# Moving six products in a feed-forward stage and reordering two accumulating transfers in a gate stage

## The chip, the cores and the metric

The kernel runs on one core of a Trainium2 chip. Such a core has a matrix engine (TensorE, PE in the profile, with its weight loads as PEld), three engines for element-wise work (VectorE or DVE, ScalarE or ACT, GpSimd or POOL), and a queue engine (SyncE or SP) that here only issues transfers. POOL also issues transfers. Every engine works through its own list of instructions in a fixed order and waits on semaphores for what others produce. The metric is the device time of one execution in microseconds (us). Three executions of the kernel before took 872.46, 872.75 and 873.51 us; the median, 872.75, is the time to compare with.

## The reference

One transformer-like layer on a sequence of 512 tokens with 1024 channels, in float32. Cut to what matters here:

```python
h = rms_norm(x, norm_mix)
u_pool, u_lru, q, k, v, g_logits = jnp.split(h @ w_in, splits, axis=-1)
gates = jax.nn.sigmoid(g_logits + b_gate).reshape(B, S, 3, D_MODEL)
merged = (gates[:, :, 0] * (y_pool @ w_branch[0])      # causal pooling mixer
          + gates[:, :, 1] * (y_lru @ w_branch[1])     # gated linear recurrence
          + gates[:, :, 2] * (y_sb @ w_branch[2]))     # stick-breaking attention
x = x + merged @ w_out
h2 = rms_norm(x, norm_ffn)
x = x + (silu(h2 @ w_ffn_gate) * (h2 @ w_ffn_up)) @ w_ffn_down
```

The change touches two places: the product that makes the third branch's gate logits (`gates[:, :, 2]`), and the first part of `silu(h2 @ w_ffn_gate) * (h2 @ w_ffn_up)`, where the feed-forward width of 2816 is worked through in 11 chunks of 256.

## The kernel before

**Precision.** Each float32 operand is split into a rounded high part and a low remainder: ACT copies the operand to the rounded type, DVE subtracts (L141 and L142, or L1442 and L1443 in the feed-forward chunks). A product is then three matmuls: high by high, high by low, low by high. So each weight tile costs one ACT and one DVE instruction before PE can use it. The split weights live in rotating buffers, three for the high and three for the low parts (`whi`, `wlo`); a fourth split waits until PE has finished with the first.

**Seven products instead of eight.** Some matrix products are done by a Strassen-like scheme: a 2x2 block product with seven block products, named 11, 12, S2, S1, S3, S4 and 22 after the weight block or sum of blocks that they use, in this order. The weight sums are made on the way. For the third branch's gate weights (two blocks, units 3 and 4 of the loader, `add_seven`), the sums are made partly by transfers: a load brings block "21", and an accumulating transfer from POOL's queue adds block "22" into it (L200). Later, when block "11" has been split and DVE has read it for another sum (L217), an accumulating transfer from POOL's queue adds "21" into the tile of "11" (L218); the result is the operand of product S3. When unit 3's block "11" has been handled, the loader also calls for unit 4's "21" and "11" (L223): SP issues the loads (L198), and POOL the addition L200 for unit 4.

**The feed-forward chunks.** The first two of the eleven chunks (`NDIRECT = 2`) use plain products with an activation that is not yet divided by its root mean square. Their results in PSUM are `pg` (gate) and `pu` (up). For each half j of a chunk, DVE multiplies `pg[j]` by 1/rms (L1513), ACT takes Silu (L1514), DVE multiplies by `pu[j]` (L1515) and by 1/rms again (L1516). The other nine chunks, `seven(c)`, use the seven-product scheme. There the weight sums S3, S2, S1 and S4 are made by DVE (L1424) from the loaded blocks, in buffers of which three rotate, and then split (L1442, L1443). `make_a(upto)` makes operands up to a count, three products ahead of the one that PE gets next: before chunk 2's first product, 11, 12 and S2 are made; S1 is made at the second product, S3 at the third, and so on. PSUM is used in four buffers of two banks each (`fp`); in chunk 2 the buffers of `pg` and `pu` of chunk 1 are the other two, and chunk 3's products take them.

**What sets the order.** The kernel is written as a program in Python, and a planner turns it into one fixed list for each engine. It simulates the engines with a cost for every instruction. Earlier instructions in the program have precedence, blocks under `tc.high_priority` more; but when an engine is free, the planner gives it what is ready by its simulation, so a later instruction that is ready can come ahead of an earlier one that is not. On the chip the list is then kept whatever the real times are. `tc.issue_after(ins)` makes the instructions of a block that go to the queue of `ins` stand behind `ins` in that list; it waits for nothing else.

Of the kernel before, what the change touches and what calls it, by code (L numbers as in the profile page):

```python
# [12 lines left out]
ALU = mybir.AluOpType  # L13
# [16 lines left out]
NDIRECT = 2  # L30
# [37 lines left out]
def layer_kernel(ctx: ExitStack, tc: tile.TileContext, x, xt, vecs, w_in, w_qkv7, w_gate7, w_pool, w_rg, w_ig,  # L68
                 w_branch, w_br7, w_out, w_fg, w_fu, w_fd, w_fd7, out):
    nc = tc.nc  # L70
# [14 lines left out]
    def b4(shape, name, tag="b", dt=F32):  # L85
        bufs = {"w": NAW, "t": NAT, "b": NAB}[tag]
        return pools["ap0"].tile([P] + shape, dt, tag=tag, name=name, bufs=bufs)
# [28 lines left out]
    def in_order2(ap):  # L116
        if ap.shape[-1] == H:
            return ap.rearrange("p w (b a) -> p w a b", a=2)
        return ap.rearrange("p w (c b a) -> p (w c) a b", c=2, a=2)

    def two2(ap):
        if ap.shape[-1] == H:
            return ap.rearrange("p w (a b) -> p w a b", a=2)
        return ap.rearrange("p w (c a b) -> p (w c) a b", c=2, a=2)
# [9 lines left out]
    def split_w(raw, shape, n, o=0):  # L134
        hi, lo = weight_tiles("whi" + n, "wlo" + n, o)
        if len(shape) == 3:
            hi, lo = (t.rearrange("p (a b) -> p a b", a=shape[1]) for t in (hi, lo))
        else:
            hi, lo = (t.rearrange("p (a b c) -> p a b c", a=shape[1], b=shape[2]) for t in (hi, lo))
        with tc.high_priority(60):  # L140
            act(hi, raw, AF.Copy)  # L141
            dve.tensor_tensor(lo, raw, hi.bitcast(F32), ALU.subtract)  # L142
        return hi, lo
# [42 lines left out]
    def seven_src(u, nm, i):  # L186
        if u < 3:
            return w_qkv7[u, CH[nm], KH[nm], i]
        return w_gate7[u - 3, CH[nm], KH[nm]]

    def seven_load(n, nms):
        if n >= len(UNITS):
            return
        u, pieces, shape = UNITS[n]
        for nm in nms:
            for i in range(pieces):
                qraw[u, nm, i] = r = b4(list(shape), f"qw{u}{nm}{i}", "w")
                nc.sync.dma_start(r, seven_src(u, nm, i))  # L198
                if nm == "21":
                    nc.gpsimd.dma_start(r, seven_src(u, "22", i), accum_op=ALU.add)  # L200

    def add_seven(un, nm, i):
        u, pieces, shape = UNITS[un]
        last = i == pieces - 1

        def make(n):
            if nm == "S4":
                r = qraw[u, "12", i]
                dve.tensor_tensor(r, r, qraw[u, "S2", i], ALU.add)
            src = qraw[u, {"S1": "21", "S3": "11", "S4": "12"}.get(nm, nm), i]  # L210
            o = 0
            if u >= 3:
                o = goffs.pop(0) if goffs else OFF
            parts = split_w(src, [P] + list(shape), n, o)
            if nm == "11":
                qraw[u, "S2", i] = r = b4(list(shape), f"qs{u}{i}")
                dve.tensor_tensor(r, qraw[u, "21", i], src, ALU.add)  # L217
                nc.gpsimd.dma_start(src, seven_src(u, "21", i), accum_op=ALU.add)  # L218
            if last:
                if un < 3:  # L220
                    seven_load(un + 1, {"S1": ("21",), "S3": ("11",), "S4": ("12",), "22": ("22",)}.get(nm, ()))
                elif un == 3:
                    seven_load(un + 1, {"11": ("21", "11"), "12": ("12",), "S2": ("22",)}.get(nm, ()))  # L223
            return parts
        specs.append((("seven", u, nm, i), make))

# [86 lines left out]
    def product(a_, b_, ps, half, first, last, ws=(0, 1)):  # L313
        for w in ws:
            o = ps[:, w, half * H:(half + 1) * H]
            for k in range(4):
                for n, (a, b) in enumerate(((0, 0), (0, 1), (1, 0))):
                    nc.tensor.matmul(o, a_[a][:, w, k, :], il2(b_[b][:, k, :]),  # L318
                                     start=first and n == k == 0,
                                     stop=last and n == 2 and k == 3, skip_group_check=True)  # L320
# [39 lines left out]
    def tick(n=1):  # L360
        for _ in range(n):
            if abg:
                abg.pop(0)()
            for _ in range(1 + (len(bg) > 8 and "many" in state)):
                if bg:
                    bg.pop(0)()
# [29 lines left out]
    def chan_chunk(key, rhs, nticks=0, pool=None, pair=False):  # L396
        pss = chunk_psum(key, pool, pair)
        for half in range(2):
            half_chunk(pss if type(pss) is list else [pss[:, j, :] for j in range(2)], key, half, rhs,
                       nticks)  # L400
        return pss
# [39 lines left out]
    with ExitStack() as first:  # L441
# [449 lines left out]
        for cc in range(2):  # L891
# [14 lines left out]
            for nm in ORDER:  # L906
                ps, half, first_, t, ts_, src, ss = plan[nm]
# [387 lines left out]
    with ExitStack() as ffn:  # L1295
        gp = ffn.enter_context(tc.tile_pool(name="gp", bufs=GBUFS))

        def g4(shape, name, dt=F32):

            return gp.tile([P] + shape, dt, tag="g", name=name)  # L1300

        def small(name, bufs=1, tag=None, dt=F32):
            return gp.tile([P, S], dt, tag=tag or name, name=name, bufs=bufs)
# [122 lines left out]
        def make_a(upto):  # L1426
            while made[0] < min(upto, len(steps)):
                c, nm = steps[made[0]]
                made[0] += 1
                if (c, nm) == (NDIRECT, "11"):  # L1430
                    offs.extend(STEPS)
                while made[1] < min(c + 2, DOWN):
                    load_a(made[1])
                    made[1] += 1
                sums_a(c, nm)
                A[c, nm] = split_a(raw[c, nm], f"{c}_{nm}")
# [30 lines left out]
        def finish_act(t, ps, a):  # L1467

            v = two2(t)
            dve.tensor_tensor(v, v, in_order2(ps), ALU.add)  # L1470
            act(t[:, 0, :], t[:, 0, :], AF.Silu)
            dve.tensor_tensor(a, t[:, 0, :], t[:, 1, :], ALU.mult)
# [4 lines left out]
        def seven(c):  # L1477
            a = g4([2, S], f"act{c}")
            tx, ty = g4([2, S], f"tx{c}"), g4([2, S], f"ty{c}")
            Y = fp.tile([P, 2, S], F32, tag="mm", name=f"ps_y{c}")  # L1480
            X = fp.tile([P, 2, S], F32, tag="mm", name=f"ps_x{c}")
            lo, hi = slice(0, H), slice(H, S)
            plan = (("11", Y, 1, True, tx, lo, Y, hi),
                    ("12", X, 0, True, None, None, None, None),
                    ("S2", Y, 1, False, tx, hi, Y, hi),
                    ("S1", X, 1, False, ty, hi, X, hi),
                    ("S3", Y, 1, False, ty, lo, Y, hi),
                    ("S4", X, 1, False, None, None, None, None),
                    ("22", Y, 0, False, None, None, None, None))
            n0 = steps.index((c, "11"))  # L1490
            for n, (nm, ps, half, first, t, ts_, src, ss) in enumerate(plan):
                make_a(n0 + n + 3)
                product(A.pop((c, nm)), B[0, WITH[nm]], ps, half, first, True)
                if t is not None:
                    act(two2(t[:, :, ts_]), in_order2(src[:, :, ss]), AF.Copy)
                if c == DOWN - 1 and nm in PRE:
                    split_d2("11", PRE.index(nm), 0, 0)
                if nm == "S4":
                    finish_act(tx, X, a[:, 0, :])
                if nm == "22":  # L1500
                    finish_act(ty, Y, a[:, 1, :])
            acts.append(a)

        bg.extend([lambda: None, rms2] + prepare_b())
        for c in range(NDIRECT):
            pg = chan_chunk(("fg", c), h2, 3, fp)
            pu = chan_chunk(("fu", c), h2, 3, fp)
            if c == NDIRECT - 1:
                make_a(3)
            a = g4([2, S], f"act{c}")  # L1510
            for j in range(2):
                sg = small(f"sg{c}{j}", 2, "sq2")
                dve.tensor_tensor(two(sg), in_order(pg[j]), two(rb2), ALU.mult)  # L1513
                act(sg, sg, AF.Silu)  # L1514
                dve.tensor_tensor(two(sg), two(sg), in_order(pu[j]), ALU.mult)  # L1515
                dve.tensor_tensor(a[:, j, :], sg, rb2, ALU.mult)  # L1516
            acts.append(a)
        tick(len(bg))
        for c in range(NDIRECT, NF // 2):
            if c == NF // 2 - 1:  # L1520
                ah, al = g4([2, S], "ah", F32R), g4([2, S], "al", F32R)
                act(ah, acts[0], AF.Copy)
                dve.tensor_tensor(al, acts[0], ah.bitcast(F32), ALU.subtract)
            seven(c)
# [207 lines left out]
```

## Time and profile before

| | us |
|---|---|
| median of 3 executions | 872.75 |
| the profiled execution | 872.6 |
| its span (first to last instruction) | 870.8 |
| PE busy in the span | 859.7 (99%) |
| DVE busy | 741.2 (85%) |
| ACT busy | 522.1 (60%) |
| POOL busy | 91.8 (11%) |

The span is divided, in order of time, into the first gates and the recurrence (to about 143 us), the attention inputs and the third branch's gates (to about 283), pooling, attention and the branch projections (to about 506), the output projection (to about 550), the feed-forward chunks (about 550 to 762) and the down projection. The gate stage of the first edit lies at 250 to 283 us, the feed-forward place of the second at 582 to 613 us.

Three things help in reading the rows. A row of a timeline gives the start, the duration, engine, line, operation and tiles, and in brackets how long the engine was idle before it and who ended that. Matmuls overlap: a matmul of 256 columns is shown with 0.28 us, but the next one starts 0.11 us later, so a loss on PE is read from the distance of starts, not from the busy time. A transfer's row on POOL or SP is only its issue; the time to landing is shown in the chain of waits or in the views of transfers.

### The profile page before, as it was taken

What the parts mean: (1) busy time and instruction counts of PE and PEld (TensorE: products, weight loads), DVE (VectorE), ACT (ScalarE), POOL (GpSimd) and SP (SyncE); (2) the same over time, 40 slices, a digit from 0 to 9 for tenths busy, and PEclk for the clock granted to TensorE, in tenths of its full rate; (3) what the DMA queues carried; (4) which work ended last, traced back from release to release, by engine and by line L of the source; (5) the groups of instructions that cost most, each with busy time, mean ns of one, the idle gap of its engine ahead of it and who ended that gap; (6) DMA issues with size and microseconds to landing.
All of it is one profiled execution on the core that took longest, in us unless ns stands there. A gap on an engine that the chain in (4) does not pass through costs nothing.

```text
span 870.8 us, 14268 instructions
## 1 busy us (share of the span) xinstructions
PE 859.7 (99%) x5563; PEld 789.7 (91%) x5563; DVE 741.2 (85%) x961; ACT 522.1 (60%) x727; POOL 91.8 (11%) x130
## 2 busy tenths in 40 slices
PE   9999999999999999999999999999999999999998
PEld 7888878888899888889889998889999999999998
DVE  7899897998787699977898786699988888899974
ACT  6554989556856565565665545464555555755642
POOL 1110002232433101000001100000000000121200
PEclk9999999999999999999999999999999999999999
DMA  9686356799582786635736955345543343798913
GB/s 340 167 291 195 97 169 194 215 318 253 176 271 73 238 246 205 218 122 155 217 98 152 212 171 170 98 138 151 150 117 97 106 114 109 233 243 204 192 39 121
DMA packets 116643, 154.08 MB, mean 177 GB/s; under 512 B 8160, under 2 KB 90080, under 8 KB 116576
## 3 DMA queue, kind: packets, MB, share of 16 engines
q1 hardware_dynamic: 103904, 107.30, 38.5%
q0 software_dynamic: 12528, 45.62, 22.1%
q8 instruction: 43, 0.70, 0.3%
q10 hardware_dynamic: 144, 0.26, 0.1%
q14 instruction: 24, 0.20, 0.1%
HBM read 132.71 MB, written 18.87 MB: 174 GB/s over the span
## 4 chain that ended last, share of the span: by engine, by line
PE 76%; DVE 10%; ACT 6%; DMA 4%; issue 2%; SPq 1%; POOL 0%; ACTq 0%; DVEq 0%; POOLq 0%
PE ps_y L318 10%; PE ps_x L318 8%; PE ps_q L834 6%; PE ps_dy L1651 6%; PE ps_dx L1651 5%; DVE wlo L142 3%; PE ps_br L309 3%; PE ps_br L310 3%; PE ps_br L311 3%; PE ps_bY L1277 2%; PE ps_gate L737 2%; DMA qw<-in_w_gate_dram 2%; PE ps_bX L1277 2%; ACT whi L141 2%; PE ps_gy L318 2%
## 5 line engine op out<-in xcount | busy, mean ns | idle before, releaser
L141 ACT ACTIVATE whi<-raw 128x1024 fp32r<-128x1024 f32 x69 | 72.8, 1055 | 76.8 <-PE ps_out L310 16.0
L142 DVE TENSOR_TENSOR wlo<-raw,whi 128x1024 fp32r<-128x1024 f32 x69 | 84.2, 1220 | 23.6 <-ACT whi L141 23.0
L142 DVE TENSOR_TENSOR wlo<-qw,whi 128x1024 fp32r<-128x1024 f32 x48 | 58.4, 1219 | 17.3 <-ACT whi L141 17.1
L141 ACT ACTIVATE whi<-qw 128x1024 fp32r<-128x1024 f32 x48 | 50.4, 1052 | 29.9 <-PE ps_q L834 14.9
L1442 ACT ACTIVATE wh_S<-w_S 128x1024 fp32r<-128x1024 f32 x36 | 38.0, 1059 | 33.0 <-PE ps_y L318 19.9
L1555 POOL DMA_DIRECT2D dw<-in_w_down_dram x20 | 16.9, 862 | 306.3 <-DMA dw<-in_w_down_dram 263.8
L1443 DVE TENSOR_TENSOR wl_S<-w_S,wh_S 128x1024 fp32r<-128x1024 f32 x36 | 43.7, 1220 | 3.8 <-ACT wh_S L1442 3.8
L1442 ACT ACTIVATE wh<-w 128x1024 fp32r<-128x1024 f32 x27 | 28.6, 1058 | 26.9 <-issue 9.1
L1443 DVE TENSOR_TENSOR wl<-w,wh 128x1024 fp32r<-128x1024 f32 x27 | 32.9, 1220 | 8.4 <-ACT wh L1442 8.4
L1442 ACT ACTIVATE whdS<-dw 128x1024 fp32r<-128x1024 f32 x20 | 21.2, 1058 | 21.3 <-PE ps_dy L1651 10.6
L1443 DVE TENSOR_TENSOR wldS<-dw,whdS 128x1024 fp32r<-128x1024 f32 x20 | 24.2, 1220 | 5.5 <-ACT whdS L1442 5.5
L1093 DVE TENSOR_TENSOR_SCAN E<-K,ahead 128x512 f32<-128x512 f32 (+3 forms) x32 | 25.3, 812 | 3.9 <-ACT K L1089 3.9
L309 PE MATMUL ps_br<-yHH,whi 128*128 128x512 f32 x64 | 24.6, 385 | 1.4 <-ACT up L980 1.4
L309 PE MATMUL ps_lru<-HH,whi 128*128 128x512 f32 x64 | 24.6, 384 | 0.0
L309 PE MATMUL ps_br<-yph,whi 128*128 128x512 f32 x64 | 24.5, 383 | 0.0
L309 PE MATMUL ps_pool<-HH,whi 128*128 128x512 f32 x64 | 24.5, 383 | 0.0
L309 PE MATMUL ps_gate<-HH,whi 128*128 128x512 f32 x64 | 24.4, 381 | 0.0
L310 PE MATMUL ps_br<-ypl,whi 128*128 128x512 f32 x64 | 24.3, 379 | 0.0
L311 PE MATMUL ps_gate<-HH,wlo 128*128 128x512 f32 x64 | 24.3, 379 | 0.0
L310 PE MATMUL ps_gate<-HL,whi 128*128 128x512 f32 x64 | 24.3, 379 | 0.0
L310 PE MATMUL ps_br<-yHL,whi 128*128 128x512 f32 x64 | 24.3, 379 | 0.0
L311 PE MATMUL ps_br<-yHH,wlo 128*128 128x512 f32 x64 | 24.3, 379 | 0.0
(740 smaller groups left out, 3444.1 us busy)
## 6 DMA issues: line engine op xcount, KB each, us to landing
raw<-in_w_in_dram SPq DMA_DIRECT2D x31, 512.0 KB, 5.1
qw<-in_w_qkv_dram SPq DMA_DIRECT2D x24, 512.0 KB, 7.0
dw<-in_w_down_dram POOLq DMA_DIRECT2D x20, 512.0 KB, 7.6
w<-in_w_ffn_gate_dram SPq DMA_DIRECT2D x36, 256.0 KB, 3.6
w<-in_w_ffn_up_dram SPq DMA_DIRECT2D x36, 256.0 KB, 4.5
raw<-in_w_branch_dram SPq DMA_DIRECT2D x16, 512.0 KB, 3.9
qw<-in_w_qkv_dram POOLq DMA_DIRECT2D x12, 512.0 KB, 8.0
qd<-r POOLq DMA_DIRECT2D x12, 512.0 KB, 7.4
```

The source lines that it names most:

```text
L141: act(hi, raw, AF.Copy)
L142: dve.tensor_tensor(lo, raw, hi.bitcast(F32), ALU.subtract)
L309: nc.tensor.matmul(ps, lh, rh, start=start, stop=False, skip_group_check=skip)
L310: nc.tensor.matmul(ps, lh, rl, start=False, stop=False, skip_group_check=skip)
L311: nc.tensor.matmul(ps, ll, rh, start=False, stop=stop, skip_group_check=skip)
L318: nc.tensor.matmul(o, a_[a][:, w, k, :], il2(b_[b][:, k, :]), start=first and n == k == 0, stop=last and n == 2 and k == 3, skip_group_che ...
L834: nc.tensor.matmul(ps[:, a, :], b_[:, k, ts_], il(a_[:, kk, :]), start=first and n == k == 0, stop=n == 2 and k == 3, skip_group_check=True)
L1093: dve.tensor_tensor_scan(E[:, c0:c0 + n][:, ::-1], K[:, c0 + 1:c0 + n + 1][:, ::-1], ahead[:, S - n:][:, ::-1], 0.0, ALU.mult, ALU.add)
L1277: nc.tensor.matmul(o, ah[x_][:, w, k, :], il2(b[k][y_]), start=first_ and n == k == 0, stop=n == 2 and k == 3, skip_group_check=True)
L1442: act(h, src, AF.Copy)
L1443: dve.tensor_tensor(l, src, h.bitcast(F32), ALU.subtract)
L1651: nc.tensor.matmul(o, a_[a][:, w, k0 + k, :], il2(b_[b][:, k, :]), start=first and i == k == 0, stop=last and i == 2 and k == nk - 1, skip ...
```

## The change

First, in the loader: where unit 3's "11" is handled, the transfers for unit 4's "21" and "11" are traced inside `tc.issue_after` of the accumulating transfer L218. So POOL's addition for the second gate block (L200) stands behind POOL's addition for the first (L218). SP's loads are not affected, being on another queue.

Second, in the feed-forward stage: the instructions that L1513 to L1516 stand for become a function of the half j, `direct_act(j)`. For chunk 0 it is called where the lines stood. For chunk 1 it is called inside `seven(2)`: for half 0 behind the second product ("12"), for half 1 behind the third ("S2"). No instruction is added or removed.

```diff
@@ in add_seven
-                nc.gpsimd.dma_start(src, seven_src(u, "21", i), accum_op=ALU.add)
+                add = nc.gpsimd.dma_start(src, seven_src(u, "21", i), accum_op=ALU.add)
             if last:
                 if un < 3:
                     seven_load(un + 1, {"S1": ("21",), "S3": ("11",), "S4": ("12",), "22": ("22",)}.get(nm, ()))
+                elif un == 3 and nm == "11":
+                    with tc.issue_after(add.ins):
+                        seven_load(un + 1, ("21", "11"))
                 elif un == 3:
-                    seven_load(un + 1, {"11": ("21", "11"), "12": ("12",), "S2": ("22",)}.get(nm, ()))
+                    seven_load(un + 1, {"12": ("12",), "S2": ("22",)}.get(nm, ()))
@@ in seven(c), end of the loop over the seven products
                     finish_act(ty, Y, a[:, 1, :])
+                if (c, n) in after:
+                    after[c, n]()
@@ the direct chunks
             a = g4([2, S], f"act{c}")
-            for j in range(2):
+
+            def direct_act(j, c=c, a=a, pg=pg, pu=pu):
                 sg = small(f"sg{c}{j}", 2, "sq2")
                 dve.tensor_tensor(two(sg), in_order(pg[j]), two(rb2), ALU.mult)
                 act(sg, sg, AF.Silu)
                 dve.tensor_tensor(two(sg), two(sg), in_order(pu[j]), ALU.mult)
                 dve.tensor_tensor(a[:, j, :], sg, rb2, ALU.mult)
+
+            if c < NDIRECT - 1:
+                direct_act(0), direct_act(1)
             acts.append(a)
         tick(len(bg))
+        after = {(NDIRECT, 1): lambda: direct_act(0), (NDIRECT, 2): lambda: direct_act(1)}
```

## The prediction

> **What bounds the kernel now.** I read the page first, for the busy engine and the clock; then the waits of TensorE (PE); then, at the two waits that the diff touches, PE's timeline, the chain of waits, and the timelines of the queues that come last there.
>
> ```profile
> span 870.8 us, 14268 instructions
> PE 859.7 (99%) x5563; PEld 789.7 (91%) x5563; DVE 741.2 (85%) x961; ACT 522.1 (60%) x727; POOL 91.8 (11%) x130
> PEclk9999999999999999999999999999999999999999
> ```
>
> The whole span is PE's at full clock. No matmul is added or removed, so the change can only remove or create moments in which PE stands still. The waits of PE, for the places that matter:
>
> ```profile
> PE ps_br L309 <- ACT up L980: 1.4, 1, 1.4
> PE ps_x L318 <- DVE wl_S L1443: 0.8, 1, 0.8
> PE ps_gy L318 <- ACT gx L910: 0.5, 1, 0.5
> ```
>
> The second row lies in the feed-forward chunk whose neighbour the diff edits, the third in the gate block whose additions it reorders. The view of waits counts idle time of a modelled span; PE's own rows give the loss in starts:
>
> ```profile
> 261.07 0.28 PE L318 MATMUL ps_gx<-hT1h,wlo 128*128 128x256 f32 x1
> 261.84 0.38 PE L318 MATMUL ps_gy<-hT3h,whi 128*128 128x256 f32 x1 [0.50 <-ACT gx L910]
> 262.06 0.28 PE L318 MATMUL ps_gy<-hT3l,whi 128*128 128x256 f32 x1
> ...
> 601.00 0.28 PE L318 MATMUL ps_y<-B0T2h,wl_S 128*128 128x256 f32 x1
> 601.40 0.38 PE L318 MATMUL ps_x<-B0T1h,wh_S 128*128 128x256 f32 x1
> 601.61 0.28 PE L318 MATMUL ps_x<-B0T1l,wh_S 128*128 128x256 f32 x1
> 602.66 0.38 PE L318 MATMUL ps_x<-B0T1h,wl_S 128*128 128x256 f32 x1 [0.77 <-DVE wl_S L1443]
> 602.87 0.28 PE L318 MATMUL ps_x<-B0T1h,wh_S 128*128 128x256 f32 x1
> ```
> ```profile
> 238.85 7.23 DMA qw<-in_w_gate_dram
> 248.72 10.48 DMA qw<-in_w_gate_dram
> 264.79 2.68 PE ps_gx L318 x24
> ```
>
> The last fence is the chain of waits from 225 to 300 us; its row of 24 matmuls gives the undisturbed step, 2.68 / 24 = 0.11 us. In the gate block two steps took 262.06 - 261.07 = 0.99 us instead of 0.22: 0.77 us lost. In the chunk four steps took 602.87 - 601.00 = 1.87 us instead of 0.44: 1.43 us lost. These two sums, 2.20 us, are all that the change can take away directly.
>
> **Edit 1, the order of two additions on POOL.** In the loader, the first gate block's "11" step adds "21" into its own tile (L218, needed for product S3). The loads for the second block follow, with an addition of their own (L200). The rows of DVE, POOL and ACT from the timeline (start, duration, line, tiles, idle time before and who ended it):
>
> ```profile
> 242.58 1.22 DVE L217 TENSOR_TENSOR qs<-qw,qw 128x1024 f32<-128x1024 f32 x1
> 246.68 0.88 POOL L200 DMA_DIRECT2D qw<-in_w_gate_dram  x1 [10.39 <-DMA qw<-in_w_gate_dram]
> 247.28 1.76 POOL L787 DMA_DIRECT2D qd<-r  x2
> 248.72 1.28 POOL L218 DMA_DIRECT2D qw<-in_w_gate_dram  x1
> 262.67 1.22 DVE L217 TENSOR_TENSOR qs<-qw,qw 128x1024 f32<-128x1024 f32 x1
> 259.30 2.00 ACT L141 ACTIVATE whi<-qw 128x1024 fp32r<-128x1024 f32 x2 [3.57 <-DMA qw<-in_w_gate_dram]
> 261.21 0.58 ACT L910 ACTIVATE gx<-ps_gy 128x512 f32<-128x512 f32 x1
> ```
>
> POOL was idle for 10.39 us ahead of L200, until the load of 238.85 had landed at 246.08; L218 had its inputs when DVE's L217 read the tile for the last time, at 242.58 + 1.22 = 243.80, and stood behind it. It went out at 248.72 and landed 10.48 later, at 259.20. ACT, in its order, waited 3.57 us for that landing, did two weight roundings, and only then the snapshot gx at 261.21, whose end releases PE's S3. From landing to PE: 261.84 - 259.20 = 2.64 us.
>
> With the edit L218 goes out at about 243.85, when POOL is idle. With the same 10.48 us it lands at 254.3. PE could go on at 261.07 + 0.11 = 261.18, which needs a landing by 261.18 - 2.64 = 258.54: 4.2 us to spare. What then ends ACT's wait is the buffer rotation, not the load. So the 0.77 us go. Behind L218 now stand L200 and the two stores L787. L200 has to wait until 246.08 for its load anyway; even if it lands 10.48 us after its old start, at 257.2, its reader, the second block's own L217 (the row at 262.67), came 5 us later. The stores are read after 290 us. SP issues the same loads in the same order and waits for nothing new. Cost nothing, gain 0.77; bounds 0 (it lands late all the same) and 0.77.
>
> ```profile
> 236.00:244.00 8.00, 8.00 (x39) 7.00 (x38) 7.09 (x7) 6.12 (x7) 0.29 (x1) 1.00 1.02 306
> 244.00:254.00 10.00, 10.00 (x63) 9.20 (x62) 9.97 (x9) 5.38 (x6) 3.96 (x5) 1.00 0.92 267
> DMA to landing us min/median/max: 5.2/7.5/11.2
> ```
>
> The first two rows are busy time by stretch (their last two numbers: share of the DMA engines, GB/s), the third belongs to the qw tile's POOL transfers. The 16 DMA engines were full when L218 would now start, so it joins a crowd; the longest landing of any such transfer was 11.2 us, and 243.85 + 11.2 = 255.1 is still before 258.54. The Trainium skill, page "DMA: Bandwidth & Descriptors", section "Issuing engines are not separate DMA queues", says that transfers issued from different engines run on the same 16 DMA engines and interleave. By that rule the earlier addition shares with SP's loads instead of going after them, which speaks against this edit; the trace agrees in so far as the share is at 1.02 with both in flight.
>
> **Edit 2, six products moved on DVE.** For chunk 1 (the second direct one) DVE did, for each half j, L1513, L1515 and L1516, with ACT's Silu between; now half 0 is queued after product "12" of chunk 2 and half 1 after "S2". None is removed. DVE before, from the timeline:
>
> ```profile
> 592.55 1.22 DVE L1424 TENSOR_TENSOR w_S<-w,w 128x1024 f32<-128x1024 f32 x1
> 593.69 0.68 DVE L1513 TENSOR_TENSOR sg<-ps_fg,rb 128x512 f32<-128x512 f32 x1
> 594.29 1.21 DVE L1424 TENSOR_TENSOR w_S<-w,w_S 128x1024 f32<-128x1024 f32 x1
> 595.42 0.68 DVE L1515 TENSOR_TENSOR sg<-sg,ps_fu 128x512 f32<-128x512 f32 x1
> 596.02 0.68 DVE L1513 TENSOR_TENSOR sg<-ps_fg,rb 128x512 f32<-128x512 f32 x1
> 596.70 1.22 DVE L1443 TENSOR_TENSOR wl_S<-w_S,wh_S 128x1024 fp32r<-128x1024 f32 x1
> 597.84 0.68 DVE L1516 TENSOR_TENSOR act<-sg,rb 128x512 f32<-128x512 f32 x1
> 598.44 0.68 DVE L1515 TENSOR_TENSOR sg<-sg,ps_fu 128x512 f32<-128x512 f32 x1
> 599.04 1.22 DVE L1424 TENSOR_TENSOR w_S<-w,w 128x1024 f32<-128x1024 f32 x1
> 600.17 0.68 DVE L1516 TENSOR_TENSOR act<-sg,rb 128x512 f32<-128x512 f32 x1
> 601.38 2.36 DVE L1443 TENSOR_TENSOR wl_S<-w_S,wh_S 128x1024 fp32r<-128x1024 f32 x2 [0.52 <-ACT wh_S L1442]
> 606.05 1.23 DVE L1443 TENSOR_TENSOR wl_S<-w_S,wh_S 128x1024 fp32r<-128x1024 f32 x1
> ```
>
> The rows L1424 are, in order, the sums for S3, S2 and S1; the last row is S4's low part. The sum for S1 starts at 599.04; its low part ends at 601.38 + 1.22 = 602.60, and PE's S1 waits for it. Five of the six products stand ahead of that sum: by differences of starts 0.60 + 0.60 + 0.68 + 0.60 + 0.60 = 3.08 us. Behind it the sum can start at 595.96, and with the same 3.56 us from its start to the low part, that is there at 599.5. PE wants it two steps after 601.11, at 601.33: 1.8 us to spare. So the 1.43 us go.
>
> What is late next? S2: its low part ended at 596.70 + 1.22 = 597.92, and PE used it 22 steps ahead of 601.11, at 598.65: 0.73 us later. While S3's sum had just ended, the planner filled with a product of 0.60; now the filler may be the sum for S1, 1.14 (592.55 to 593.69). That eats 0.54, and 0.2 is left: no wait. If ACT also rounds S1 before S2 (1.0 by the row of two at 259.30), S2 comes 0.8 us late, which is the lower bound: a gain of 0.63. S4: its low part ended at 606.05 + 1.23 = 607.28, and PE's use lies 47 steps of 0.112 behind 602.87, at 608.12; 1.43 earlier is 606.69, so 0.59 is lacking if DVE gains nothing. But the work that DVE owes by then is the same, and it loses the 0.52 of idleness ahead of 601.38. So S4's wait is between 0 and 0.59 us; I take 0, the nearer end by that row. From chunk 3 on DVE has room:
>
> ```profile
> 632.00:650.70 18.70, 18.70 (x170) 18.70 (x169) 16.52 (x16) 10.63 (x13) 0.00 (x0) 1.00 0.41 114
> ```
>
> DVE is busy 16.52 of 18.70 us in a chunk, so what is still owed (at most the six products, 3.7 us) is paid back within two. The two Silu, on ACT, are free: 10.63 of 18.70. L1516's result is read first in the last chunk, far behind. SP and POOL issue nothing here that moves: the loads of chunks 2 and 3 stand ahead of the products as before. Gain 1.43, bounds 0.63 and 1.43.
>
> **Sum.** 0.77 + 1.43 = 2.20 us. The profiled execution took 872.6 us (span 870.8 and 1.8 around it), 0.15 under the median of 872.75. So 870.4 for such an execution, 870.55 for the median: 870.6. After each wait PE runs on the rotation of weight buffers behind itself, so I let the whole shift reach the end.
>
> **Rivals.**
> - *A new wait of S2 or S4 takes part of it.* For it: the margins of 0.2 and about 0 just worked out, and a planner that fixes each engine's order ahead. Against: 1.8 us to spare for S1. Time: 872.75 - 0.77 - 0.7 = 871.3 (0.7 being a gain near the lower bound).
> - *The products do not move.* The planner also fills by readiness, and these are ready early; if it places them as before, only edit 1 counts: 872.0. Against: the sum for S1 now stands ahead of them in the program, and its inputs are there.
> - *The addition lands late in the crowd.* With the engines full, its packets take turns with three of SP's loads. It would have to take over 14.7 us from 243.85 (to 258.54) instead of at most 11.2; then up to 0.77 stays: 871.3. This is what the rule on issuing engines of the page "DMA: Bandwidth & Descriptors" of the Trainium skill would do here.
> - *Slower: a PSUM bank is held.* Four two-bank buffers serve these chunks; chunk 3's first product takes the one that L1513 of half 1 (or L1515) frees. They were last read at 598.44 + 0.68 = 599.12. Chunk 3 starts 46 steps behind 608.12, at 613.26, so now near 611.8. If the planner lets the moved products sink behind all other work that is ready, PE stops there; DVE then has at most the low parts of the three weight buffers (3 x 1.14 = 3.4) and the two L1513 (1.2) to do before the bank is free: 4.6 us, 872.75 - 2.2 + 4.6 = 875.2. It decides once the last read ends after 611.8 + 2.2 = 614.0. Against: the products stand ahead of S4's and all of chunk 3's sums in the program.
>
> A changed simulated time also lets the planner reorder far work; the wait of 1.4 at L980 shows what one bad order costs, either way. That widens the range below and above.
>
> **How the numbers follow.** Both edits whole: 0.52, 870.2 to 871.0. New wait of S2 or S4: 0.20. Products unmoved: 0.12. Late landing: 0.06. Bank held or far reordering for the worse: 0.10. The forecast is 870.6; 869.8 to 872.4 takes in the first four cases, with 0.4 below the first for reordering. 0.2% is 1.75 us (about what a measurement of this kernel can tell from no change), so faster means under 871.0: the first case and a little of the second, 0.55; same 0.36; slower 0.09.
>
> **What would show it.** L218 ahead of L200 on POOL, landing before 258; no gap in PE's starts at S3 of the first gate block. The sum for S1 on DVE before 597, no DVE wait of PE at S1 of chunk 2; L1513 and L1515 of half 1 done before 610. The prediction is wrong if PE waits anew at S2 or S4 of chunk 2 or at chunk 3's first product, or if waits elsewhere, as at L980, change by a microsecond.

## The result and the profile after

The changed kernel took 871.87 us (median of 22 executions, 870.82 to 873.63), the kernel before 872.89 (22, 871.64 to 875.47). The ratio is 0.9985 with a 95% interval of 0.9979 to 0.9991, so 1.3 us less, between 0.8 and 1.8. That is real, and within 0.2%. The forecast was 2.2 us less. Below, "before" and "after" are the two kernels; the lines behind the loader have numbers that are 3 to 10 higher in the kernel after (L1443 is now L1446, L910 is L913, L980 is L983, L1495 is L1498, L787 is L790, L1513 to L1516 are L1519 to L1522).

The profiled execution of the kernel after took 872.3 us. Its page:

```profile
span 870.5 us, 14271 instructions
PE 860.6 (99%) x5563; PEld 790.0 (91%) x5563; DVE 741.1 (85%) x961; ACT 523.1 (60%) x727; POOL 91.2 (10%) x130
PEclk9999999999999999999999999999999999999999
```

PE still fills the span at full clock. The span is only 0.3 us shorter than that of the trace of before; why this one pair of executions shows so little is a part of what follows. Two rows of the waits of PE:

```profile
PE ps_br L312 <- ACT up L983: 1.4, 1, 1.4
...
PE ps_y L321 <- ACT tx L1498: 0.2, 1, 0.2
```

The waits for `wl_S` and for `gx` are gone, the far wait at L983 is as it was (1.4), and one row is new: PE waits for a snapshot `tx` of ACT. PE's own rows at the places of the change (timeline of the kernel after):

```profile
261.64 0.28 PE L321 MATMUL ps_gx<-hT1h,wlo 128*128 128x256 f32 x1
261.76 0.28 PE L321 MATMUL ps_gy<-hT3h,whi 128*128 128x256 f32 x1
261.87 0.28 PE L321 MATMUL ps_gy<-hT3l,whi 128*128 128x256 f32 x1
...
601.08 0.28 PE L321 MATMUL ps_y<-B0T2h,wl_S 128*128 128x256 f32 x1
601.19 0.28 PE L321 MATMUL ps_x<-B0T1h,wh_S 128*128 128x256 f32 x1
...
601.41 0.28 PE L321 MATMUL ps_x<-B0T1h,wl_S 128*128 128x256 f32 x1
...
603.76 0.28 PE L321 MATMUL ps_x<-B0T1h,wl_S 128*128 128x256 f32 x1
604.22 0.38 PE L321 MATMUL ps_y<-B0T3h,wh_S 128*128 128x256 f32 x1 [0.18 <-ACT tx L1498]
604.43 0.28 PE L321 MATMUL ps_y<-B0T3l,wh_S 128*128 128x256 f32 x1
```

At S3 of the gate block (261.76) every start is 0.11 behind the last one, and at S1 of chunk 2 (601.19) three steps take 0.33: both waits are gone. At S3 of chunk 2 two steps take 604.43 - 603.76 = 0.67 us instead of 0.22: 0.45 us are lost at a place where before lost nothing.

What stands ahead of that stop, from the timelines of DVE and ACT of the kernel after:

```profile
593.75 0.69 DVE L1519 TENSOR_TENSOR sg<-ps_fg,rb 128x512 f32<-128x512 f32 x1
595.48 1.22 DVE L1427 TENSOR_TENSOR w_S<-w,w 128x1024 f32<-128x1024 f32 x1
597.22 1.22 DVE L1446 TENSOR_TENSOR wl_S<-w_S,wh_S 128x1024 fp32r<-128x1024 f32 x1
598.95 1.22 DVE L1446 TENSOR_TENSOR wl_S<-w_S,wh_S 128x1024 fp32r<-128x1024 f32 x1
600.69 0.68 DVE L1521 TENSOR_TENSOR sg<-sg,ps_fu 128x512 f32<-128x512 f32 x1
601.29 1.22 DVE L1427 TENSOR_TENSOR w_S<-w,w_S 128x1024 f32<-128x1024 f32 x1
602.62 1.06 ACT L1445 ACTIVATE wh_S<-w_S 128x1024 fp32r<-128x1024 f32 x1 [1.91 <-DVE w_S L1427]
603.59 0.58 ACT L1498 ACTIVATE tx<-ps_y 128x512 f32<-128x512 f32 x1
605.29 1.22 DVE L1446 TENSOR_TENSOR wl_S<-w_S,wh_S 128x1024 fp32r<-128x1024 f32 x1
```

S1's sum starts at 595.48, ahead of S2's low part (597.22), and S1's low part is there at 600.17. The first of the six products (593.75) stands where it stood. S4's sum, at 601.29, is the new end of the line: ACT idles 1.91 us for it, rounds S4, and only then copies S2's half of `ps_y` to `tx` (603.59 to 604.17). S3 writes to that same half, so PE waits for the copy. In the kernel before, ACT's list had these two the other way round:

```profile
602.20 0.58 ACT L1495 ACTIVATE tx<-ps_y 128x512 f32<-128x512 f32 x1
604.96 1.06 ACT L1442 ACTIVATE wh_S<-w_S 128x1024 fp32r<-128x1024 f32 x1 [2.19 <-DVE w_S L1424]
```

The change made S4's sum 2.4 us earlier (601.29 against 603.65). In the planner's simulation it presumably now came ahead of the end of product S2, so that ACT got the rounding first; no run shows the simulated times themselves.

The gate stage, DVE and POOL of the kernel after:

```profile
242.40 0.73 POOL L790 DMA_DIRECT2D qd<-r  x1 [5.84 <-DVE r L854]
247.68 1.22 DVE L142 TENSOR_TENSOR wlo<-qw,whi 128x1024 fp32r<-128x1024 f32 x1
248.07 0.73 POOL L790 DMA_DIRECT2D qd<-r  x1 [4.93 <-DVE r L854]
249.21 0.93 POOL L218 DMA_DIRECT2D qw<-in_w_gate_dram  x1 [0.41 <-DVE wlo L142]
249.81 1.23 POOL L200 DMA_DIRECT2D qw<-in_w_gate_dram  x1
```

And the view of line L218 of the kernel after, for its one transfer:

```profile
DMA to landing us min/median/max: 6.8/6.8/6.8
```

L218 is ahead of L200, as the change wants. But it went out at 249.21, no earlier than before (248.72): it waits for DVE's low part of the "11" block itself, which ends at 247.68 + 1.22 = 248.90. What is new is the way to the landing: 6.8 us instead of 10.48, so it lands at 256.0 instead of 259.20. Two transfers that went out within 3 us ahead of it before no longer do: L200 now stands behind it, and one of the two stores (L787 before, L790 here) goes out at 242.40, because it no longer stands behind L200, which waited for its load. Each of them moves 512 KB.

### The profile page after: what moved, and what is told of

Its sections match the earlier page's. It is cut to its first block, busy times and chain, and to the rows that moved or that the text cites. A ratio compares the mean times of both kernels' runs of the same rounds, so it can differ in the third digit from the quotient of the medians.

```text
span 870.5 us, 14271 instructions
## 1 busy us (share of the span) xinstructions
PE 860.6 (99%) x5563; PEld 790.0 (91%) x5563; DVE 741.1 (85%) x961; ACT 523.1 (60%) x727; POOL 91.2 (10%) x130
## 4 chain that ended last, share of the span: by engine, by line
PE 84%; DVE 7%; ACT 5%; DMA 2%; issue 1%; SPq 0%; ACTq 0%; DVEq 0%
PE ps_y L321 11%; PE ps_x L321 8%; PE ps_q L837 7%; PE ps_dy L1661 6%; PE ps_dx L1661 5%; PE ps_br L312 3%; PE ps_br L313 3%; PE ps_br L314 3%; PE ps_bY L1280 2%; PE ps_gate L740 2%; PE ps_gy L321 2%; DVE wlo L142 2%; PE ps_bX L1280 2%; PE ps_gx L321 2%; PE ps_lru L312 1%; PE ps_out L312 1%
## 5 line engine op out<-in xcount | busy, mean ns | idle before, releaser
L142 DVE TENSOR_TENSOR wlo<-raw,whi 128x1024 fp32r<-128x1024 f32 x69 | 84.3, 1221 | 24.8 <-ACT whi L141 24.3
L142 DVE TENSOR_TENSOR wlo<-qw,whi 128x1024 fp32r<-128x1024 f32 x48 | 58.4, 1220 | 16.5 <-ACT whi L141 16.3
L1446 DVE TENSOR_TENSOR wl_S<-w_S,wh_S 128x1024 fp32r<-128x1024 f32 x36 | 43.9, 1221 | 3.2 <-ACT wh_S L1445 3.2
L1446 DVE TENSOR_TENSOR wl<-w,wh 128x1024 fp32r<-128x1024 f32 x27 | 33.0, 1221 | 8.2 <-ACT wh L1445 8.2
L1446 DVE TENSOR_TENSOR wldS<-dw,whdS 128x1024 fp32r<-128x1024 f32 x20 | 24.2, 1222 | 4.9 <-ACT whdS L1445 4.9
L313 PE MATMUL ps_lru<-HL,whi 128*128 128x512 f32 x64 | 24.3, 379 | 0.0
L314 PE MATMUL ps_lru<-HH,wlo 128*128 128x512 f32 x64 | 24.3, 379 | 0.0
L313 PE MATMUL ps_pool<-HL,whi 128*128 128x512 f32 x64 | 24.3, 379 | 0.0
## 6 DMA issues: line engine op xcount, KB each, us to landing
w<-in_w_ffn_gate_dram SPq DMA_DIRECT2D x36, 256.0 KB, 3.7
w<-in_w_ffn_up_dram SPq DMA_DIRECT2D x36, 256.0 KB, 4.2
```

What stands on the lines that cost most here:

```text
L313: nc.tensor.matmul(ps, lh, rl, start=False, stop=False, skip_group_check=skip)
L314: nc.tensor.matmul(ps, ll, rh, start=False, stop=stop, skip_group_check=skip)
L1446: dve.tensor_tensor(l, src, h.bitcast(F32), ALU.subtract)
```

## The experiments

The runs came in three groups; each kernel of a group ran on the same chip beside executions of the kernel before. All times and ratios:

| run | median us | ratio to before | 95% interval |
|---|---|---|---|
| after, second | 871.85 | 0.9983 | 0.9974 to 0.9992 |
| addition alone (e1) | 872.61 | 0.9997 | 0.9988 to 1.0006 |
| products alone (e2) | 871.90 | 0.9990 | 0.9981 to 0.9998 |
| snapshot first (e3) | 871.21 | 0.9978 | 0.9968 to 0.9987 |
| before, second | 873.11 | 1.0005 | 0.9996 to 1.0014 |
| after, third | 872.17 | 0.9991 | 0.9982 to 1.0000 |
| snapshot first, again | 871.09 | 0.9982 | 0.9973 to 0.9991 |
| products still later (e4) | 871.24 | 0.9985 | 0.9976 to 0.9994 |
| before, third | 872.75 | 0.9999 | 0.9991 to 1.0008 |
| after, fourth | 871.73 | 0.9985 | 0.9977 to 0.9994 |
| before, fourth | 872.76 | 0.9998 | 0.9990 to 1.0007 |
| after, fifth | 871.74 | 0.9989 | 0.9980 to 0.9997 |

The theory (A) was read from the first pair of traces: the two waits go, 0.45 comes back at the snapshot, and the rest is lost between 786 and 799 us because PE arrives there early. Its rival (B): the stop there was of that one execution.

### The changed kernel again, and each edit alone

> The changed kernel once more, as the base for the three runs beside it. Theory A (an account by places): the wait at S3 of the gate block (0.77 us) and the one at S1 of chunk 2 (1.43) are gone, 0.45 comes back at S3 of chunk 2, where TensorE waits for the snapshot tx behind S4's rounding on ACT, and some 0.6 comes back between 786 and 799 us, where the down projection's loads set the pace. So again about 1 us under before, with the same two new stops in the trace. Rival B: the stop in the down projection was of that one execution; then 1.7 to 1.8 us under before (0.77 + 1.43 - 0.45) and no loss between 786 and 799.

Edit 1 alone is the first hunk of the diff without the rest:

```diff
+                add = nc.gpsimd.dma_start(src, seven_src(u, "21", i), accum_op=ALU.add)
...
+                elif un == 3 and nm == "11":
+                    with tc.issue_after(add.ins):
+                        seven_load(un + 1, ("21", "11"))
```

> Only the two additions' order on POOL is changed, chunk 2 is as before. A: no gap at S3 of the gate block (0.77 gone), the 1.43 at S1 of chunk 2 stays, TensorE reaches the down projection at most 0.77 us early and keeps a third to all of it: 0.2 to 0.77 under before. B: 0.77 under before. A third way, that the gate block's gain is lost at the transposes of the q loads at 299 us (0.2 came back there): 0.57 under before.

Edit 2 alone is the rest without that hunk:

```diff
+                if (c, n) in after:
+                    after[c, n]()
...
+        after = {(NDIRECT, 1): lambda: direct_act(0), (NDIRECT, 2): lambda: direct_act(1)}
```

> Only the products of the second direct chunk are queued later, the additions are as before. A: the 0.77 at S3 of the gate block stays; S1's 1.43 gone, the snapshot's 0.45 there; TensorE reaches the down projection 1.0 us early and keeps a third to all of it: 0.3 to 1.0 under before. B: 1.0 under before. If the whole shift of 1.43 reached the end and the stop at the snapshot cost nothing: 1.4.

Measured: 0.9983, 0.9997 and 0.9990. By the ratios that is 1.5, 0.3 and 0.9 us. Edit 2 gives what its places say: its trace has no wait at S1 and the snapshot's stop, 1.43 - 0.45 = 1.0. Edit 1, whose trace shows no gap at S3 of the gate block, measures 0.3 us and not 0.77; but its interval (1.05 less to 0.5 more) holds both, and nothing too. The second trace of after loses 0.24 between 786 and 799, not 0.63.

### Is the gate wait always 0.77 us?

> The kernel before once more, for a second trace of it. The first matmuls of the gate began 0.1 to 1.0 us later in the five traces since than in the trace shown of before, whatever the kernel. If that is chance of the first loads, this trace starts late as well, by 0.1 to 1.0 us at 12 us into the span; if it comes from the changed text, it starts as before, within 0.1. The waits at S3 of the gate block (0.77) and S1 of chunk 2 (1.43) must be there again. Ratio 1.000.

> What is open: by places the changed kernel should be 1.75 us under before (0.77 + 1.43 - 0.45), measured are 1.2. Its three traces lost 0.2, 0.0 and 0.65 at the transposes at 299 us and 0.63, 0.1 and 0.1 between 786 and 799, against the first trace of before; the second trace of before lost 0.13 and 0. If these stops are chance of loads that land late, a third and a fourth trace of before show one of 0.2 us or more at one of the two places, and the gap is a matter of few runs. If they come from the change, before shows none.

> As for the third trace of before: chance, a stop of 0.2 us or more at 299 or between 786 and 799 in one of the two; from the change, none in either.

The first matmuls of the gate start 0.8 us late in the second trace of before, 0.35 in the third and not at all in the fourth, so that is chance of the first loads. The wait at S1 is there in all three, 1.4 us. The wait at S3 of the gate block, expected at 0.77, is there at 0.22, 0.14 and 0. PE's rows of the fourth trace of before:

```profile
261.05 0.28 PE L318 MATMUL ps_gx<-hT1h,wlo 128*128 128x256 f32 x1
261.16 0.28 PE L318 MATMUL ps_gy<-hT3h,whi 128*128 128x256 f32 x1
261.28 0.28 PE L318 MATMUL ps_gy<-hT3l,whi 128*128 128x256 f32 x1
```

The same from edit 2 alone, which has the old order on POOL, with its row of the chain of waits:

```profile
248.76 10.86 DMA qw<-in_w_gate_dram
```
```profile
261.20 0.28 PE L318 MATMUL ps_gx<-hT1h,wlo 128*128 128x256 f32 x1
262.27 0.38 PE L318 MATMUL ps_gy<-hT3h,whi 128*128 128x256 f32 x1 [0.79 <-ACT gx L910]
262.48 0.28 PE L318 MATMUL ps_gy<-hT3l,whi 128*128 128x256 f32 x1
```

Nothing is lost in the one, 262.48 - 261.20 - 0.22 = 1.06 us in the other. The five traces with the old order, read the same way:

| trace | L218 out | to landing | S3's first matmul | lost there |
|---|---|---|---|---|
| before | 248.72 | 10.5 | 261.84 | 0.77 |
| before, second | 249.51 | 9.9 | 262.09 | 0.22 |
| before, third | 249.01 | 9.9 | 261.60 | 0.14 |
| before, fourth | 248.61 | 9.5 | 261.16 | 0 |
| products alone | 248.76 | 10.9 | 262.27 | 1.06 |

Wherever something is lost, S3's first matmul follows the landing by the 2.64 us that the prediction found (259.62 + 2.64 = 262.26). The landing itself moves by more than a microsecond from one execution to the next, and PE's own arrival by 0.8: in the second trace of before the landing (259.45) is later than in the first (259.20), yet less is lost, because PE, late since the first loads, reaches S3 0.8 us later. The mean loss of the four traces of before is 0.28 us; with the trace of edit 2 alone, whose gate stage is the same, it is 0.44. The 0.3 that edit 1 alone measures fits either. In the nine traces with the new order the transfer takes 6.3 to 7.4 us and nothing is lost.

### The snapshot ahead of S4's rounding

In chunk 2 the rounding for S4 is queued behind the snapshot. ACT's two instructions change places; nothing else moves.

```diff
-                make_a(n0 + n + 3)
+                with tc.issue_after(snap.ins) if (c, n) == (NDIRECT, 3) else ExitStack(): make_a(n0 + n + 3)
...
-                    act(two2(t[:, :, ts_]), in_order2(src[:, :, ss]), AF.Copy)
+                    snap = act(two2(t[:, :, ts_]), in_order2(src[:, :, ss]), AF.Copy)
```

> As the changed kernel, but in chunk 2 ACT takes the snapshot of S2 ahead of the rounding for S4; these two instructions change places and nothing else moves. A: ACT, which idles 1.9 us ahead of that rounding, takes the snapshot at about 601.5, the stop of 0.45 us at S3 is gone; S4's low part is there at 606.5 and is wanted at 606.7, so no new stop. TensorE reaches the down projection 0.45 earlier and loses most of it there again: 0 to 0.2 under the changed kernel. B: 0.45 under the changed kernel.

> The snapshot of S2 ahead of S4's rounding, once more, to see the size: 0.45 under the changed kernel and 2.2 under before if every shift reaches the end (B); 1.3 to 1.5 under before if the down projection takes back what comes early (A).

Measured: 871.21 and 871.09, 0.6 and 1.1 us under the changed kernel of the same group, 1.9 and 1.6 under before by the ratios. ACT and PE in the first of the two traces:

```profile
601.35 0.60 ACT L1498 ACTIVATE tx<-ps_y 128x512 f32<-128x512 f32 x1 [0.66 <-PE ps_y L321]
602.57 1.06 ACT L1445 ACTIVATE wh_S<-w_S 128x1024 fp32r<-128x1024 f32 x1 [0.61 <-DVE w_S L1427]
```
```profile
603.72 0.28 PE L321 MATMUL ps_x<-B0T1h,wl_S 128*128 128x256 f32 x1
603.83 0.28 PE L321 MATMUL ps_y<-B0T3h,wh_S 128*128 128x256 f32 x1
```

The snapshot now runs in the time in which ACT only waited, the rounding starts when it did (602.57), and S3 follows S1 without a gap. The one thing left is a step of 0.21 instead of 0.11 at S2 of chunk 3 (617.24 to 617.45), right behind the next snapshot; so 0.1 of the gain is lost there. PE gets to the down projection earlier than in any trace of after, and loses nothing between 786 and 799 in either trace. The fourth trace of before, too, gets there earlier (first matmul on the tiles `Bd111` at 775.49) than the fifth of after (776.16), and only the latter loses time. So theory A, that an early arrival is what costs time there, falls. This version has the lowest medians of all, though its intervals overlap those of after and e4.

### The products still later

```diff
-        after = {(NDIRECT, 1): lambda: direct_act(0), (NDIRECT, 2): lambda: direct_act(1)}
+        after = {(NDIRECT, 3): lambda: direct_act(0), (NDIRECT, 5): lambda: direct_act(1)}
```

> The two calls of the products are put behind products S1 and S4 of chunk 2 instead of behind 12 and S2. ACT's order stays: S4's rounding ahead of the snapshot. On DVE the last product of each half (by 1/rms) now goes behind S4's sum, the others stay. If the snapshot is late because S4's sum stood behind that product (0.60 us by differences of starts), the sum, the rounding and the snapshot come 0.6 us earlier, TensorE's stop of 0.45 at S3 goes, and the time is 2.2 under before, as with the snapshot put first. If ACT's order alone makes the stop, it stays at 0.45 and the time is that of the changed kernel. S4's low part, now behind one more sum, would be there at about 606.5 and is wanted at 606.7; if it is late, up to 0.5 comes back at S4.

Measured: 871.24, ratio 0.9985. DVE, ACT and PE in its trace:

```profile
600.09 1.21 DVE L1427 TENSOR_TENSOR w_S<-w,w_S 128x1024 f32<-128x1024 f32 x1
602.38 0.58 ACT L1498 ACTIVATE tx<-ps_y 128x512 f32<-128x512 f32 x1
...
607.15 0.69 DVE L1522 TENSOR_TENSOR act<-sg,rb 128x512 f32<-128x512 f32 x1
607.75 1.22 DVE L1446 TENSOR_TENSOR wl<-w,wh 128x1024 fp32r<-128x1024 f32 x1
```
```profile
603.15 0.28 PE L321 MATMUL ps_x<-B0T1h,wl_S 128*128 128x256 f32 x1
603.26 0.28 PE L321 MATMUL ps_y<-B0T3h,wh_S 128*128 128x256 f32 x1
...
608.73 0.28 PE L321 MATMUL ps_y<-B0T4l,wh 128*128 128x256 f32 x1
609.03 0.38 PE L321 MATMUL ps_y<-B0T4h,wl 128*128 128x256 f32 x1
609.24 0.28 PE L321 MATMUL ps_y<-B0T4h,wh 128*128 128x256 f32 x1
```

S4's sum comes 1.2 us earlier, of which PE's own earlier arrival (S1 at 600.58 against 601.19) is 0.6. The other 0.6 is the L1522 that no longer stands ahead of it. With ACT's order unchanged the snapshot ends at 602.96, ahead of S3 at 603.26: the stop is gone. So the stop needs both ACT's order and the 0.6 us of a product ahead of S4's sum; to remove either is enough. The stop feared at S4 did not come. Instead the L1522 at 607.15 now stands ahead of the low part of the next block, "22", which ends at 608.97; there 609.24 - 608.73 - 0.22 = 0.29 us are lost. That, the 0.1 in chunk 3, a loss in the down projection (below) and the smaller gate wait make up, by places, what is missing from the 2.2 under before that was expected.

### The stops at 299 and between 786 and 799

> The changed kernel a third time. If TensorE's early arrival at the down projection is what costs time there (theory A), 0.3 us or more is lost again between 786 and 799; if the loads landed late in that one execution (B), nothing or about 0.1 is lost, as in the second trace. Time 1.0 to 1.8 us under before; the stop of 0.45 at S3 of chunk 2 is there in any case.

> The changed kernel beside it. Chance: losses at the two places like those of before in the same call, 0 to 0.7 in all, and a difference of the times of 1.0 to 1.8 us. From the change: 0.3 us or more lost at the two places together each time, and a difference of 1.0 to 1.4.

> As for the fourth trace of the changed kernel: chance, 0 to 0.7 us lost at the two places in all; from the change, 0.3 or more.

Between 786 and 799 the five traces of after lost 0.63, 0.24, 0.24, 0.24 and 0.47 us, the four of before nothing. So 0.24 of it is of the kernel, not of an execution: more than B's 0.1 and less than A's 0.3. (The 0.1 that the expectations give for the second and third trace counts one of the two long steps below; both together are 0.24.) The third trace's time, 0.8 us under before, also lies outside the 1.0 to 1.8 that was expected, with an interval of 0 to 1.6. PE's rows of the fourth trace of after:

```profile
786.52 0.27 PE L1661 MATMUL ps_dx<-Bd120l,whd 128*128 128x256 f32 x1
786.76 0.38 PE L1661 MATMUL ps_dx<-Bd120h,wld 128*128 128x256 f32 x1
786.98 0.28 PE L1661 MATMUL ps_dx<-Bd120h,whd 128*128 128x256 f32 x1
```

These two steps take 0.46 instead of 0.22. It starts ten microseconds earlier on ACT; the fourth rounding `whd` of the stage, in the fourth trace of after and then in the fourth of before:

```profile
776.10 1.06 ACT L1445 ACTIVATE whd<-dw 128x1024 fp32r<-128x1024 f32 x1 [1.99 <-PE ps_dy L1661]
```
```profile
775.63 1.06 ACT L1442 ACTIVATE whd<-dw 128x1024 fp32r<-128x1024 f32 x1 [1.70 <-PE ps_dy L1651]
```

Measured from PE's first matmul on the tiles `Bd111` it starts 0.41 us later in all five traces of after and in e4, and 0.14 later in the eight others (before, e1, e2, e3). The instruction with which ACT waits ahead of it ends 0.09 us behind that matmul in all fourteen, so by these records neither PE nor a transfer makes the difference: it lies on ACT, between the end of the wait and the start of the rounding (0.05 us in the eight, 0.32 in the six). DVE's low parts behind it are late by the same 0.27, and PE feels it at 786. The rest of the first and the fifth trace (0.4 and 0.2), and 0.2 more in e4, is a load that landed late (5.5 to 5.7 us from issue, 3.8 to 5.0 in the others), in the first one:

```profile
792.36 1.06 ACT L1445 ACTIVATE whd<-dr 128x1024 fp32r<-128x1024 f32 x1 [4.95 <-DMA dr<-in_w_down_dram]
```

At 299 us, where PE transposes loaded `at` tiles, the five traces of after stood 0.2, -0.05, 0.65, 0.8 and 1.05 us against the first trace of before, the other three of before at +0.13, -0.1 and -0.15, edit 2 alone at +1.6, and e1, e3 and e4 between -0.2 and +0.2. Where it is long (0.6 or more), a weight load ahead of the `at` loads on SP landed late, 6.2 to 7.7 us from issue instead of 4.7 to 5.3. Edit 2 alone (waits of PE, then the view of that load):

```profile
PE pq L1056 <- DMA at<-qd: 1.5, 1, 1.5
```
```profile
DMA to landing us min/median/max: 7.7/7.7/7.7
```

In the second trace of e3 the same load took 5.1 us. The expectation "chance" is not met in the way it was put, since no trace of before shows it; but e3 and e4, whose lists of instructions up to there are those of after, do not show it either. Edit 2 alone, with the old order on POOL, has the longest. Whether the changed kernel meets it more often is open.

### The sum by places

Taken from the kernel before (mean gate loss 0.28, S1's loss 1.4), and set beside the ratios, in us:

| kernel | gate S3 | S1 | snapshot | later | sum | measured |
|---|---|---|---|---|---|---|
| addition alone | -0.28 | 0 | 0 | 0 | -0.3 | -0.3 |
| products alone | 0 | -1.4 | +0.45 | 0 | -0.95 | -0.9 |
| after | -0.28 | -1.4 | +0.45 | +0.24 | -1.0 | -0.8 to -1.5 (five times) |
| snapshot first | -0.28 | -1.4 | 0 | +0.1 | -1.6 | -1.9, -1.6 |
| products still later | -0.28 | -1.4 | 0 | +0.29 + 0.1 + 0.24 | -1.05 | -1.3 |

All agree within their intervals, without the stop at 299. The intervals are wide, 0.5 us to either side for the first measurement and 0.8 for the others, so they would hold a gate term of 0.77 as well; what speaks for less are the traces. That the stop at 299 leaves no trace in the timed executions as a rule is seen in the profiled ones: those of after took 0.45, -0.1, 0.3, 0.4 and 1.1 us more than the median of the executions beside them, with stops of 0.2, -0.05, 0.65, 0.8 and 1.05, and that of edit 2 alone 1.8 more, with a stop of 1.6. It also answers why the first pair of traces differs by only 0.3 us: that of after started 0.5 late at the first loads, and lost 0.2 at 299 and 0.63 in the down projection, which leaves little of the 0.77 and 1.0 that it gained.

## Why the prediction was right, and where it was not

- *PE bounds the whole span, and the two waits are all that the change can take.* Right: the rows at both places close up, and nothing else on PE got faster by the change. That it can also add waits, the prediction said, and some came: at the snapshot, in the down projection and, with the products still later, at "22".
- *Edit 1, L218 goes out at about 243.85.* Wrong. The step took DVE's L217 (ending at 243.80) for the last reader of the "11" tile; the low part of that tile (L142, ending at 248.90 after) reads it too, and L218 waits for that, in both orders. The addition went out when it always did. The wait went all the same, for a reason that the prediction does not have, and that is luck: the landing took 6.3 to 7.4 us instead of 9.5 to 10.9. The two stores do not stand behind L218 either; both go out ahead of it, one of them 5 us earlier than before. So of the three transfers of 512 KB that went out within 3 us ahead of L218, one is left. Before, they land one after the other, L200 at 254.2, the stores at 255.5 and 256.8 and L218 at 259.2; after, L218 lands at 256.0 and L200 at 258.5. Which part of the 3 to 4 us belongs to L200 and which to the store, no run separates. The third rival had the crowd on the wrong side: what had been late was the old order. It rests on the Trainium skill, page "DMA: Bandwidth & Descriptors", section "Issuing engines are not separate DMA queues", which says that transfers issued by different engines interleave on the same 16 DMA engines. As L218 never went out into the crowd of SP's loads at 243.85, no run here shows what that would have cost; what the runs show is the wait behind transfers of POOL's own queue.
- *Gain 0.77; bounds 0 and 0.77.* The term was mis-sized. One execution showed 0.77; the four traces of before have 0.77, 0.22, 0.14 and 0, so 0.28 in the mean (0.44 with the 1.06 of edit 2 alone). The path from landing to PE (2.64 us) and the landing that PE needs (258.5) were right; the scatter of the landing, over a microsecond in five traces, and of PE's own arrival was not considered. That ACT's wait then ends with the rotation of buffers was right as well: after, PE ends it.
- *Edit 2, S1's sum at 595.96, gain 1.43.* Right in size: 595.48, and 1.4 in every trace. The order behind it is another: one of the five products (593.75) still stands ahead of the sum, and S2's low part has gone behind it instead. The low part of S1 came at 600.17 instead of 599.5, with two moved products and S2's low part between, still 1.2 ahead of the 601.41 at which PE used it.
- *What is late next: S2 with 0.2 to spare, S4 with 0 to 0.59, taken as 0.* Right for both: no wait at either; S2's low part ended at 598.44, and PE used it at 598.73, 0.3 later. The step failed by what it left out. It followed the low parts on DVE only, and not the snapshots on ACT, whose list can be turned round when a sum comes earlier. The 0.45 us at S3 are the first rival's mechanism (a new wait in chunk 2 takes part of the gain) at another product; at 0.45 instead of 0.7.
- *The two Silu are free, a held PSUM bank is possible.* Right: `ps_fu` was last read at 600.69 + 0.68 = 601.37, ten microseconds ahead of chunk 3, and the fourth rival did not happen. Nor did the second: five of the six products moved.
- *"I let the whole shift reach the end."* Right for the version with the snapshot first but for 0.1 us in chunk 3, and off by 0.24 us for the changed kernel, which loses that in the down projection.

So the forecast of 870.6 was 1.3 under the measured 871.87, of which by these places 0.5 is the gate term, 0.45 the snapshot and 0.24 the down projection. Against before in the same measurement, 1.3 less instead of 2.2, it is only 0.9 off, with an uncertainty of 0.5. The range held it because it was drawn to the cases of a new wait.

## What to carry to other kernels

A wait that ends with a transfer's landing has a size that one trace cannot give: read it from several executions before it goes into a sum. When a change makes an operand ready sooner, look at every engine that handles it next: a planner may put its next step ahead of something that others need more urgently, and two instructions exchanged by hand then give the rest of the gain. Ahead of claiming that an instruction can go out sooner, look for all readers of its tile, not only for the one beside it in the text.

## What the runs showed of the hardware

The same accumulating transfer of 512 KB, in the same place of the same program, took 9.5 to 10.5 us to land in four executions, and 6.4 to 6.8 in five executions of the changed kernel, where another addition and a store of 512 KB each no longer went out within 3 us ahead of it on the same queue. In two kernels, after and e4, one rounding on ACT starts 0.27 us later than in the other four in every trace, although ACT's wait ahead of it ends at the same point in all (0.09 us behind one matmul) and the instructions of that stage are the same in e3 and in after; what makes the difference was not found.
